# A bias table built with copies on GpSimd instead of matmuls on TensorE

## The chip, the cores and the metric

One core of a Trainium2 chip runs the whole program. The metric is device time in microseconds (us); the time before is the median of three runs. Engines are named as in the profile: PE is TensorE (PEld its weight loads), DVE VectorE, ACT ScalarE, POOL GpSimd, and SP the sync engine, whose queue issues nearly all of this kernel's DMAs.

## The reference

A bidirectional encoder of two layers works on 256 tokens of width 1024. Each layer has a token mixer and a gated MLP. The mixer projects the normed tokens to pooling channels, queries, keys, values and gates. Attention has three groups of four heads with strides 1, 4 and 16; each group adds a bias by relative position, in T5 buckets, the same in both layers. Cut to what the change touches:

```python
def _t5_buckets(rel):                       # 32 buckets
    n = -rel
    half = N_BUCKETS // 2
    ret = (n < 0).astype(np.int32) * half
    n = np.abs(n)
    max_exact = half // 2
    large = max_exact + (np.log(np.maximum(n, 1) / max_exact)
                         / np.log(MAX_DISTANCE / max_exact) * (half - max_exact)).astype(np.int32)
    large = np.minimum(large, half - 1)
    return (ret + np.where(n < max_exact, n, large)).astype(np.int32)
...
    for gi, (window, dilation) in enumerate(ATTN_GROUPS):
        hs = slice(gi * HEADS_PER_GROUP, (gi + 1) * HEADS_PER_GROUP)
        half = window // (2 * dilation)
        buckets = _t5_buckets(dilation * np.arange(-half, half + 1))
        bias = rel_bias[buckets][:, hs].T
        o_g, lse_g = _dilated_group(q[:, :, hs], k[:, :, hs], v[:, :, hs], bias, window, dilation)
```

In `_dilated_group` the bias is added to the logits, and positions outside the window or the sequence are set to -1e30.

## The kernel before

Tokens are held as two sets of 128, even and odd ones. All big products run on PE with each weight split into a high part (cast by ACT, line 177 or 185) and a rest (subtracted by DVE, line 178 or 186), in pieces. Class `Weights` keeps the order of the pieces. A DMA of 1 MB (line 117, tile `raw`, three buffers) loads two pieces; `W.get` splits up to three pieces ahead, with five buffers of split pieces; a raw buffer comes free when its second piece is split, and then the next load can go.

The program text of layer 0 has this order: the values of x (lines 654 and 741, first piece groups scaled by the norm's gain on the way), the parameters (`load_params`, lines 341 to 350), the bias table (`load_bias`, then the generator `build_bias`), the gain of norm2 (line 290), eight pooling projections (line 484) with their window sums on DVE (lines 814 to 836), the query and key projections, with the pooling output `pool_ps` among them, and the attention steps. The text's order is a priority only: a scheduler orders each engine's instructions and each queue's DMAs by its own reckoning of when their data is ready. `tc.issue_after(ins)` adds, to each instruction traced in the block on the engine of `ins`, an edge behind it; `W.behind[1]` is a DVE instruction, the last scaled subtraction of the first stage.

POOL does little: in each norm it adds up the sums of squares and takes the power that gives `rstd` (lines 423 to 428, in the first norm 628 to 631). Line 719 spreads that `rstd` over partitions with PE (`r_ps`).

**The bias table.** Head h and distance kind n (five kinds: even to even, two odd ones, stride 4, stride 16) need, for each of 255 distances, the bias of its bucket or a large negative number. `_bias_table` holds 33 rows of 5 x 256: row b has a 1 where bucket b applies, row 32 the mask. Before, these 33 rows come in by a DMA (`onehot_sb`), ACT casts them (`ohr`), the 32 x 12 biases come in as `rb` with a 33rd row of ones, DVE splits them into `rh` and `rl`, and PE multiplies: two matmuls of 4 x 256 for each kind into `f_ps` (line 374), copied by DVE to `fsb` (line 378). A `yield` follows each kind, and each pooling projection of layer 0 calls `next(bias)` first, so that one kind stands before each of the first five projections and the rest before the sixth:

```python
        fd = dram.tile([1, n], F32, name="fd")
        nc.sync.dma_start(out=fd[0].rearrange("(h e) -> h e", h=HPG), in_=fsb)
        sk = dram.tile([P, n + 1], F32, name="sk")
        nc.sync.dma_start(out=sk[:, 0:n], in_=fd[0].partition_broadcast(P))
```

This is the way through DRAM (lines 383 and 385): the 20 KB go to `fd`, then 128 times to `sk` (2.5 MB), and five DMAs (line 390) read them back with a row pitch that shifts each partition by one, into `bt`, which the scores read (line 885, first at 112.5 us).

Three tags of the pool `big` matter: `m2` holds pieces of the first values, then `ohr`, then `po2` and `m2`; `ybig` and `q1` held `onehot_sb` and `fsb` between other tiles.

Of the kernel before, what the change touches and what calls it, by code (L numbers as in the profile page):

```python
# [10 lines left out]
F32 = mybir.dt.float32  # L11
F32R = mybir.dt.float32r
# [4 lines left out]
P = 128  # L17
# [5 lines left out]
HPG = 4  # L23
NG = 3
NH = HPG * NG
# [8 lines left out]
NT = 5  # L34
# [10 lines left out]
def _buckets(rel):  # L45
    n = -rel
    ret = (n < 0).astype(np.int32) * 16
    n = np.abs(n)
    large = 8 + (np.log(np.maximum(n, 1) / 8) / np.log(1024 / 8) * 8).astype(np.int32)
    large = np.minimum(large, 15)  # L50
    return (ret + np.where(n < 8, n, large)).astype(np.int32)


def _bias_table():

    t = np.zeros((33, NT, 256), np.float32)
    delta = np.arange(255) - 127
    for n, (e, dil) in enumerate(
        ((2 * delta, 1), (2 * delta + 1, 1), (2 * delta - 1, 1), (2 * delta, 4), (2 * delta, 16))
    ):  # L60
        valid = (e % dil == 0) & (np.abs(e) <= 64 * dil)
        b = _buckets(e)
        j = np.nonzero(valid)[0]
        t[b[j], n, j] = 1.0
        t[32, n, np.nonzero(~valid)[0]] = NEG
        t[32, n, 255] = NEG
    return t.reshape(33, NT * 256)


def _edge_table():  # L70
# [134 lines left out]
def encoder(ctx, tc, x, w_in, w_pool, pool_scale, w_a, w_b, w_o, norm1, norm2, w_up, conv_w,  # L205
            conv_b, w_down, rel_bias, norm_f, onehot, edges, out):
    nc = tc.nc
    const = ctx.enter_context(tc.tile_pool(name="const", bufs=1))
    wpool = ctx.enter_context(tc.tile_pool(name="weights", bufs=1))
    big = ctx.enter_context(tc.tile_pool(name="big", bufs=1))  # L210
    sm = ctx.enter_context(tc.tile_pool(name="small", bufs=2))
    acc = ctx.enter_context(tc.tile_pool(name="acc", bufs=4, space=bass.MemoryType.PSUM))
# [6 lines left out]
    def cols(w, c0):  # L219

        src = w[:, c0 : c0 + 256].rearrange("(k p) c -> p k c", p=P)
        return W.add(
            src, (8, 256), [((lambda t, j=j: t[:, :, j * P : (j + 1) * P]), (8, P)) for j in (0, 1)]
        )
# [10 lines left out]
    for l in range(DEPTH):  # L235
        for g in range(NG):
            c0 = C_V + g * 512
            slots = (("m2", 0, 2), ("m2", 1, 2), ("ybig",), ("at2",)) if g == 0 else ()
            for j in range(2):
                tag = "k1" if l == 0 and g == 1 and j == 0 else None  # L240
# [34 lines left out]
        for f in range(0, NF, 2):  # L275
            a = cols(w_up[l], f * P) if f >= ENTRY else []
            g = cols(w_up[l], DFF + f * P)
# [7 lines left out]
    h = const.tile([P, 2, D], F32, name="h")  # L285
    xv = x[0].rearrange("(m t) d -> m t d", t=2)

    def gain(src):
        g = sm.tile([P, D], F32, tag="gain", bufs=1, name="gain")
        nc.sync.dma_start(out=g, in_=src.partition_broadcast(P))  # L290
        return g
# [47 lines left out]
    def load_params():  # L339

        nc.sync.dma_start(out=edge.rearrange("p a b -> p (a b)"), in_=edges[0].partition_broadcast(P))
        for l in range(DEPTH):
            rowst = sm.tile([96, P], F32, tag="s", name="prow")
            nc.sync.dma_start(out=rowst[0:66, :], in_=conv_w[l].rearrange("w (f p) -> (w f) p", p=P))
            nc.sync.dma_start(out=rowst[66:88, :], in_=conv_b[l].rearrange("(f p) -> f p", p=P))
            nc.sync.dma_start(out=rowst[88:96, :], in_=pool_scale[l].rearrange("(f p) -> f p", p=P))
            pt = mmp.tile([P, 512], F32, tag="mm", name="prm_ps")
            nc.tensor.transpose(pt[:, :96], rowst, ident[:96, :96])
            nc.vector.tensor_copy(prm[:, l, :], pt[:, :96])
            nc.vector.tensor_scalar_mul(hps[:, l, :], prm[:, l, 88:96], 0.5)  # L350

    bt = const.tile([P, HPG, NT * P], F32, name="bt")

    def load_bias():
        oh = big.tile([33, NT * 256], F32, tag="ybig", name="onehot_sb")
        nc.sync.dma_start(out=oh, in_=onehot)
        rb = sm.tile([33, NH], F32, tag="rb", bufs=1, name="rb")
        nc.vector.memset(rb, 1.0)
        nc.sync.dma_start(out=rb[0:32, :], in_=rel_bias)
        rh = sm.tile([33, NH], F32R, tag="ms", name="rh")  # L360
        rl = sm.tile([33, NH], F32R, tag="ms", name="rl")
        nc.vector.tensor_copy(rh, rb)
        nc.vector.tensor_sub(out=rl, in0=rb, in1=rh.bitcast(F32))
        ohr = big.tile([33, NT * 256], F32R, tag="m2", name="onehot_r")
        nc.scalar.copy(out=ohr, in_=oh)
        return rh, rl, ohr

    def build_bias(rh, rl, ohr):

        fsb = big.tile([HPG, NT * 256], F32, tag="q1", name="fsb")  # L370
        for n, g in enumerate((0, 0, 0, 1, 2)):
            ps = acc.tile([P, 512], F32, tag="acc", name="f_ps")
            for j, r in enumerate((rh, rl)):
                nc.tensor.matmul(
                    ps[:HPG, :256], r[:, g * HPG : (g + 1) * HPG], ohr[:, n * 256 : (n + 1) * 256],
                    start=(j == 0), stop=(j == 1),
                )
            nc.vector.tensor_copy(fsb[:, n * 256 : (n + 1) * 256], ps[:HPG, :256])
            yield

        n = HPG * NT * 256
# [4 lines that stand above are left out]
        for blk, kind in enumerate((2, 0, 1, 3, 4)):  # L386
            src = bass.AP(
                sk.tensor, sk.offset + kind * 256 + 127, [[n, P], [NT * 256, HPG], [1, P]]
            )
            nc.sync.dma_start(out=bt[:, :, blk * P : (blk + 1) * P], in_=src)  # L390
        yield
# [179 lines left out]
    def v_tile():  # L571
        return acc.tile([P, 512], F32, tag="acc", name="v_ps")
# [176 lines left out]
    for l in range(DEPTH):  # L749
# [25 lines left out]
        else:  # L775
            for g in range(NG):
                held = begun[0] if g == 0 else [W.get() for _ in range(4)]
                for t in range(2):
                    if g + t == 0:
                        ps = begun[1]  # L780
                    else:
                        ps = v_tile()
# [6 lines left out]
        if l == 0:  # L789
            load_params()  # L790
            with tc.issue_after(W.behind[1].ins):
                bias = build_bias(*load_bias())
        g2 = gain(norm2[l])


# [4 lines left out]
        for gi in range(3, -1, -1):  # L800
# [8 lines left out]
            cur, n = u, S + 2 * PAD  # L809
            sh = 1  # L810
            while sh < w:
# [3 lines left out]
                    out=nxt[:, :, 0:n], in0=cur[:, :, 0:n], in1=cur[:, :, sh : sh + n]  # L815
# [7 lines left out]
            if hw > 1:  # L823
                e = edge[:, gi, hw : w - 1].unsqueeze(1).to_broadcast([P, 2, hw - 1])
                r = slice(o + S - hw + 1, o + S)
# [3 lines left out]
                out=pd, in0=cur[:, :, o : o + S], scalar=1.0 / w, in1=u[:, :, PAD : PAD + S],  # L829
# [108 lines left out]
        for pair in ((0, 1), (2, 3)):  # L938
            a, b = pair
# [8 lines left out]
        for m, c in enumerate(PAIRS):  # L948
# [7 lines left out]
            for n in range(4):  # L956
# [5 lines left out]
                if hd < HPG:  # L962
# [3 lines left out]
                        out=lo[:, hd], in0=src, scalar=scale, in1=hi[:, hd].bitcast(F32),  # L966
# [3 lines left out]
                        out=lo[:, hd], in0=rest, scalar=scale, in1=lo[:, hd].bitcast(F32),  # L970
                        op0=ALU.mult, op1=ALU.add,
                    )
                else:
# [3 lines left out]
                        out=o, in0=src, scalar=scale, in1=o, op0=ALU.mult, op1=ALU.add  # L977
# [20 lines left out]
        for c in range(KD):  # L998
            th = gate(c)
            nc.vector.scalar_tensor_tensor(  # L1000
                out=pa[:, c, :], in0=th, scalar=1.0, in1=pa[:, c, :], op0=ALU.add, op1=ALU.mult
            )
        m2 = big.tile([P, 2, KD, 2, P], F32R, tag="m2", name="m2")
        mh, ml = m2[:, 0], m2[:, 1]
        for c4 in range(2):
            ths = [gate(4 * c4 + j) for j in range(4)]
            for j2 in range(2):
                i, (wh, wl) = W.get()
                for j in range(2):
                    c = 4 * c4 + 2 * j2 + j  # L1010
                    ps = mmp.tile([P, 2, S], F32, tag="mm", name="b_ps")
# [5 lines left out]
                        out=m, in0=ths[2 * j2 + j], scalar=1.0, in1=m, op0=ALU.add, op1=ALU.mult  # L1017
# [49 lines left out]
        held, ps = entry  # L1067
        first = keep_entry(ps)
        ps = v_tile()
# [106 lines left out]
```

## Time and profile before

| | before |
|---|---|
| median of three runs | 880.66 us (880.24 to 880.85) |
| the profiled execution | 880.48 us, of which span 878.7 us |
| granted TensorE clock | 0.998 |
| PE busy | 870.6 us, 4817 matmuls |
| DVE busy | 684.3 us, 1167 instructions |
| ACT busy | 524.1 us, 929 instructions |
| POOL busy | 14.1 us, 40 instructions |
| f_ps (line 374) | 10 matmuls, 43.5 to 55.2 us |
| fd, sk, first bt issued | 56.98, 60.89, 74.55 us |

The span runs from the first to the last instruction; the run's time has 1.78 us more around it. In the views, a line gives the start or the busy time in us, the engine, the line of the kernel, the operation, out<-in and a count; a bracket is idle time before it and what ended that. PEld is the weight load of a matmul and overlaps PE. A time of a DMA issue on SP (SPq) is that of the issuing, not of the transfer.

### The profile page before, as it was taken

The numbers are of one execution on the slowest core, as the hardware profiler recorded it, in microseconds if no ns is written. First come the engines' busy times: TensorE is split into PE (matmuls) and PEld (weight loads), VectorE is DVE, ScalarE is ACT, GpSimd is POOL, SyncE is SP. The second block draws the span as 40 slices with busy tenths as digits, with TensorE's granted clock in tenths as the row PEclk, the third lists the DMA queues.
The fourth block names the chain that finished last, engine by engine and source line by source line (L and its number), as shares of the span: only waits on it lengthen the run. The fifth ranks groups of instructions, "written<-read, shape, count | busy, mean of one in ns | idle before, by whom it ended". The sixth has DMA issues, their size and how long they took to land.

```text
span 878.7 us, 12698 instructions
## 1 busy us (share of the span) xinstructions
PE 870.6 (99%) x4817; PEld 756.5 (86%) x4817; DVE 684.3 (78%) x1167; ACT 524.1 (60%) x929; POOL 14.1 (2%) x40
## 2 busy tenths in 40 slices
PE   9999999999999999999999999999999999999996
PEld 7888889988888888888888888899888888888885
DVE  7987886766869987787755987776678698877874
ACT  7745654556647766666545565554666486656662
POOL 2000000000000000000000000000000000000000
PEclk9999999999999999999999999999999999999999
DMA  9669744454565465465636465443556447456441
GB/s 336 229 204 290 261 145 149 140 186 158 187 211 194 143 239 193 145 232 198 240 120 223 161 197 187 149 162 125 188 191 213 152 151 252 168 192 212 171 144 49
DMA packets 125790, 164.47 MB, mean 187 GB/s; under 512 B 2995, under 2 KB 106107, under 8 KB 125600
## 3 DMA queue, kind: packets, MB, share of 16 engines
q1 hardware_dynamic: 125712, 163.65, 55.5%
q8 instruction: 38, 0.62, 0.3%
q14 instruction: 24, 0.20, 0.1%
q10 hardware_dynamic: 16, 0.00, 0.0%
HBM read 162.57 MB, written 3.69 MB: 189 GB/s over the span
## 4 chain that ended last, share of the span: by engine, by line
PE 99%; ACT 0%; issue 0%; POOL 0%; DVE 0%; POOLq 0%; ACTq 0%
PE proj_ps L484 61%; PE v_ps L579 6%; PE res_ps L510 6%; PE res_ps L511 6%; PE res_ps L509 6%; PE b_ps L484 3%; PE v_ps L741 2%; PE v_ps L654 1%; PE pool_ps L484 1%; PE s_ps L879 1%; PE o_ps L929 1%; PE pt_ps L908 1%; PE s_ps L874 1%; PE o_ps L925 1%; PE xt_ps L450 1%; PE gain_ps L333 0%
## 5 line engine op out<-in xcount | busy, mean ns | idle before, releaser
L178 DVE TENSOR_TENSOR wl<-raw,wh 128x1024 fp32r<-128x1024 f32 x274 | 334.0, 1223 | 87.1 <-ACT wh L177 85.0
L484 PE MATMUL proj_ps<-x,wh 128*128 128x512 f32 x1408 | 360.0, 393 | 0.0
L177 ACT CAST wh<-raw 128x1024 fp32r<-128x1024 f32 x274 | 286.4, 1050 | 80.4 <-PE res_ps L511 39.1
L484 PEld LDWEIGHTS proj_ps<-x,wh 128*128 128x128 f32 x1408 | 257.5, 188 | 47.3 <-issue 0.7
L484 PEld LDWEIGHTS proj_ps<-x,wl 128*128 128x128 f32 x1408 | 192.6, 190 | 10.6
L484 PE MATMUL proj_ps<-x,wl 128*128 128x256 f32 x1408 | 196.7, 283 | 0.0
L509 PE MATMUL res_ps<-wh,actq 128*128 128x512 f32 (+1 forms) x184 | 70.0, 380 | 0.0
L510 PE MATMUL res_ps<-wl,actq 128*128 128x512 f32 (+1 forms) x184 | 69.9, 380 | 0.0
L511 PE MATMUL res_ps<-wh,actk 128*128 128x512 f32 (+1 forms) x184 | 69.9, 380 | 0.0
L1089 ACT ACTIVATE y<-a,prm 128x256 f32<-128x256 f32 x36 | 21.6, 601 | 40.3 <-DVE a L505 40.3
L509 PEld LDWEIGHTS res_ps<-wh,actq 128*128 128x128 f32 x184 | 34.6, 188 | 6.6
L510 PEld LDWEIGHTS res_ps<-wl,actq 128*128 128x128 f32 x184 | 34.6, 188 | 6.6
L511 PEld LDWEIGHTS res_ps<-wh,actk 128*128 128x128 f32 x184 | 34.6, 188 | 6.5
L484 PE MATMUL proj_ps<-po,wh 128*128 128x512 f32 x128 | 34.0, 400 | 0.0
L1090 DVE SCALAR_TENSOR_TENSOR y<-a,prm,y 128x255 f32<-128x255 f32 x36 | 17.4, 483 | 14.2 <-ACT y L1089 14.2
L484 PEld LDWEIGHTS proj_ps<-po,wh 128*128 128x128 f32 x128 | 23.1, 189 | 3.9
L509 PE MATMUL res_ps<-wh,m 128*128 128x512 f32 (+1 forms) x72 | 26.5, 368 | 0.0
L511 PE MATMUL res_ps<-wh,m 128*128 128x512 f32 (+1 forms) x72 | 26.3, 365 | 0.0
L510 PE MATMUL res_ps<-wl,m 128*128 128x512 f32 (+1 forms) x72 | 26.3, 365 | 0.0
L579 PE MATMUL v_ps<-wh,x 128*128 128x512 f32 x80 | 25.7, 392 | 0.0
L416 ACT ACTIVATE junk<-h 128x512 f32<-128x512 f32 (+1 forms) x20 | 10.9, 546 | 24.7 <-DVE h L414 24.7
L995 ACT ACTIVATE gates<-gates 128x256 f32<-128x256 f32 x32 | 13.1, 415 | 18.9 <-DVE gates L505 18.9
(208 smaller groups left out, 1111.0 us busy)
## 6 DMA issues: line engine op xcount, KB each, us to landing
raw<-in_w_in_dram SPq DMA_DIRECT2D x58, 1024.0 KB, 5.6
raw<-in_w_up_dram SPq DMA_DIRECT2D x44, 1024.0 KB, 5.1
raw<-in_w_down_dram SPq DMA_DIRECT2D x22, 1024.0 KB, 5.0
raw<-in_w_a_dram SPq DMA_DIRECT2D x8, 1024.0 KB, 5.1
raw<-in_w_o_dram SPq DMA_DIRECT2D x8, 1024.0 KB, 5.0
raw<-in_w_b_dram SPq DMA_DIRECT2D x4, 1024.0 KB
sk<-fd SPq DMA_DIRECT2D x1, 2560.0 KB
raw<-in_w_pool_dram SPq DMA_DIRECT2D x2, 1024.0 KB
```

Source lines behind the costliest of these rows:

```text
L177: lambda: nc.scalar.copy(out=h, in_=src),
L178: lambda: nc.vector.tensor_sub(out=l, in0=src, in1=h.bitcast(F32)),
L416: nc.scalar.activation(junk[:, 0 : cc.stop - cc.start], h[:, t, cc], AF.Square, scale=D**-0.5, accum_out=ss[:, n : n + 1],)
L484: nc.tensor.matmul(out, w(k), x, start=(n == 0), stop=(n == 2 * nk - 1))
L509: nc.tensor.matmul(ps, ah, wh, start=first, stop=False)
L510: nc.tensor.matmul(ps, ah, wl, start=False, stop=False)
L511: nc.tensor.matmul(ps, al, wh, start=False, stop=last)
L579: nc.tensor.matmul(ps, x2[:, 2 * n + j, part, t, :], w[:, j, :], start=(n + m == 0), stop=(n == 3 and m == 5),)
L741: nc.tensor.matmul(ps[t], a[:, k, t, :], w[:, j, :], start=(k + m == 0), stop=(k == KD - 1 and m == 2),)
L995: nc.scalar.activation(th, th, AF.Tanh, scale=0.5)
L1089: nc.scalar.activation(y, a, AF.Identity, bias=b, scale=w1)
L1090: nc.vector.scalar_tensor_tensor(out=y[:, 1:], in0=a[:, : S - 1], scalar=w0, in1=y[:, 1:], op0=ALU.mult, op1=ALU.add)
```

## The change

The matmuls that build the table, their inputs and their copies go. Instead the biases are loaded turned, four heads on four partitions (`rbt`, three small DMAs), and row 32, the mask, is loaded onto the four partitions of `fsb`. POOL then copies, for each run of places that share a bucket, that bucket's bias over the run: 15, 16, 15 and 11 runs in the kinds 0, 1, 3 and 4, of 1 to 22 elements; kind 2 is one copy of kind 1, moved by a place. `fsb` lies in `m2` instead of `q1`. The generator now yields six times, the first of them taken at once, so that the way through DRAM stands before the sixth pooling projection in the text as it did before.

```diff
+def _runs(n):
+
+    t = _bias_table()[:32].reshape(32, NT, 256)[:, n]
+    runs = []
+    for b in range(32):
+        places = np.nonzero(t[b])[0]
+        if len(places):
+            step = int(places[1] - places[0]) if len(places) > 1 else 1
+            assert (np.diff(places) == step).all()
+            runs.append((b, int(places[0]), len(places), step))
+    return runs
...
-    def load_bias():
-        oh = big.tile([33, NT * 256], F32, tag="ybig", name="onehot_sb")
-        nc.sync.dma_start(out=oh, in_=onehot)
-        rb = sm.tile([33, NH], F32, tag="rb", bufs=1, name="rb")
-        nc.vector.memset(rb, 1.0)
-        nc.sync.dma_start(out=rb[0:32, :], in_=rel_bias)
-        rh = sm.tile([33, NH], F32R, tag="ms", name="rh")
-        rl = sm.tile([33, NH], F32R, tag="ms", name="rl")
-        nc.vector.tensor_copy(rh, rb)
-        nc.vector.tensor_sub(out=rl, in0=rb, in1=rh.bitcast(F32))
-        ohr = big.tile([33, NT * 256], F32R, tag="m2", name="onehot_r")
-        nc.scalar.copy(out=ohr, in_=oh)
-        return rh, rl, ohr
-
-    def build_bias(rh, rl, ohr):
-
-        fsb = big.tile([HPG, NT * 256], F32, tag="q1", name="fsb")
-        for n, g in enumerate((0, 0, 0, 1, 2)):
-            ps = acc.tile([P, 512], F32, tag="acc", name="f_ps")
-            for j, r in enumerate((rh, rl)):
-                nc.tensor.matmul(
-                    ps[:HPG, :256], r[:, g * HPG : (g + 1) * HPG], ohr[:, n * 256 : (n + 1) * 256],
-                    start=(j == 0), stop=(j == 1),
+    def build_bias():
+        rbt = sm.tile([HPG, NG, 32], F32, tag="rb", bufs=1, name="rbt")
+        fsb = big.tile([HPG, NT, 256], F32, tag="m2", name="fsb")
+        for g in range(NG):
+            with nc.allow_non_contiguous_dma("a small table, turned"):
+                nc.sync.dma_start(
+                    out=rbt[:, g], in_=rel_bias[:, g * HPG : (g + 1) * HPG].rearrange("b h -> h b")
                 )
-            nc.vector.tensor_copy(fsb[:, n * 256 : (n + 1) * 256], ps[:HPG, :256])
+        nc.sync.dma_start(
+            out=fsb.rearrange("p a b -> p (a b)"), in_=onehot[32].partition_broadcast(HPG)
+        )
+        for n, g in ((0, 0), (1, 0), (3, 1), (4, 2)):
+            for b, j, count, step in _runs(n):
+                nc.gpsimd.tensor_copy(
+                    fsb[:, n, j : j + (count - 1) * step + 1 : step],
+                    rbt[:, g, b : b + 1].to_broadcast([HPG, count]),
+                )
+
+        nc.gpsimd.tensor_copy(fsb[:, 2, 64:192], fsb[:, 1, 63:191])
+        fsb = fsb.rearrange("p a b -> p (a b)")
+        for _ in range(6):
             yield
...
             load_params()
             with tc.issue_after(W.behind[1].ins):
-                bias = build_bias(*load_bias())
+                bias = build_bias()
+                next(bias)
```

## The prediction

> **What bounds the kernel now.** I read the page first: engine shares and the chain that ended last.
>
> ```profile
> span 878.7 us, 12698 instructions
> PE 870.6 (99%) x4817; PEld 756.5 (86%) x4817; DVE 684.3 (78%) x1167; ACT 524.1 (60%) x929; POOL 14.1 (2%) x40
> PE 99%; ACT 0%; issue 0%; POOL 0%; DVE 0%; POOLq 0%; ACTq 0%
> ```
>
> PE is never without work once it has started, so an edit gains by what it takes out of PE's order and loses by any hole it tears there. POOL is almost unused. Next I read the chain in order of time around the bias build (start, length, what).
>
> ```profile
> 41.91 1.62 PE proj_ps L484 x7
> 43.54 0.32 PE f_ps L374 x2
> ...
> 45.56 2.99 PE proj_ps L484 x16
> 48.54 0.33 PE f_ps L374 x2
> ...
> 55.16 0.32 PE f_ps L374 x2
> 55.48 22.50 PE proj_ps L484 x128
> ...
> 79.38 2.79 PE proj_ps L484 x16
> ```
>
> The five f_ps pairs are on the path, and a projection beside one takes 2.97 to 2.99 us where an undisturbed one takes 2.79. Third, the DMA queue of SP, in order of time (start, length, issue).
>
> ```profile
> 20.79 0.36 SPq L290 DMA_DIRECT2D gain<-in_norm_dram  x1
> ...
> 55.48 0.37 SPq L117 DMA_DIRECT2D raw<-in_w_pool_dram  x1
> 56.98 0.28 SPq L383 DMA_DIRECT2D fd<-fsb  x1
> 60.89 0.59 SPq L385 DMA_DIRECT2D sk<-fd  x1
> 63.94 0.39 SPq L117 DMA_DIRECT2D raw<-in_w_in_dram  x1
> 74.55 3.28 SPq L390 DMA_DIRECT2D bt<-sk  x5
> 77.94 32.74 SPq L117 DMA_DIRECT2D raw<-in_w_in_dram  x9
> ```
>
> Two things are to be seen. The way through DRAM (fd, sk, bt) holds SP from 57 to 78 us with one weight load let through. And SP's order is not the order of the program text: the gain of norm2 stands behind the whole value stage in the text (PE ends that at 41.7) and goes out at 20.79. The scheduler puts a transfer where it reckons its data ready.
>
> Last, what POOL does beside DVE (all engines, around 435 us).
>
> ```profile
> 434.44 1.23 DVE L178 TENSOR_TENSOR wl<-raw,wh 128x1024 fp32r<-128x1024 f32 x1 [0.69 <-ACT wh L177]
> 435.11 0.63 POOL L423 TENSOR_SCALAR ss<-ss 128x1 f32<-128x1 f32 x1 [176.18 <-ACT junk L416]
> 437.26 0.19 POOL L425 TENSOR_TENSOR ss<-ss 128x1 f32<-128x1 f32 x1 [1.52 <-ACT junk L416]
> 437.53 0.57 POOL L428 TENSOR_TENSOR rstd<-ss,mhalf 128x1 f32<-128x1 f32 x1
> ```
>
> The L423 instruction takes 0.22 us when DVE is idle (250.04, 440.94). Here it took 0.63 and ended at 435.74, 0.07 after DVE's subtraction of two SBUF operands (435.67). At 10.31 two of them took 2.01 us beside such DVE work. So a POOL instruction waits out a DVE instruction that reads two SBUF operands; DVE's own 1.23 is its usual length.
>
> **What is removed.** Ten matmuls in five places. From the first projection (41.91) to 55.48 are 13.57 us with 64 projection matmuls; at 2.79 for 16 these cost 11.16. The five pairs therefore cost 2.41 us, 1.61 as f_ps and 0.80 in the changeovers; with the slower pace of the next stretch (22.50 for 128) it is 2.32. I take 2.4. Also gone are DVE's five copies (0.41 each), its memset, cast and subtraction (0.4), and ACT's cast of 1.26: all beside PE, counted at nothing, since the weights they could hasten are split 8 us ahead there (the piece split until 55.41 is used by the projection of about 63.9). The onehot and rb loads go too.
>
> **What is added on SP.** Three small turned loads and the mask row, for two loads removed: two issues more, at 0.28 to 0.42 us each, 0.7 us. They fall before 23.92, ahead of which SP waits 2.8 us for a free raw buffer (gain's issue ends at 21.15): nothing, and 0.7 if that cover were gone. Their transfers are small; what the element-wise reads cost is between 0 and some microseconds of a few DMA engines, against first use of raw loads of that time at 32.5. I take nothing.
>
> **What is added on POOL.** 15, 16, 15 and 11 runs of a bucket and one copy: 58 instructions. No copy is in this trace. Bounds for one: 0.03 us apart (the constant memsets at the start) and 0.97 (the mean of L628); the nearest rows are L425, 0.20 long, and L425 to L428, 0.28 from start to start. I take 0.20, and 0.10 (the memsets' length) and 0.28 as ends. They start at about 25.5: the mask issued at about 21.5 and 3.6 to 3.9 to land, as fd and the gain show. From 25.5 to 56.6 DVE spends 21.4 us in two-operand SBUF instructions (L186 5.5, L178 9.8, L729 2.6, L814 2.8, L828 0.7), 25 of them, which leaves 9.6 us. Letting POOL take one copy behind each such instruction and the beat in the free stretches, the 58 are done at 40 (0.10), 49 (0.20) or 56 us (0.28). I take 49. At 0.97 it would be 82. If each copy held DVE up for the 0.07 seen above, that would be 58 x 0.07 = 4 us of DVE, of which PE would feel what its lead doesn't cover, 0 to 4; the DVE rows beside POOL show no lengthening, so I take 0.
>
> The Trainium skill, GPSIMD Engine Reference, Specifications, says that POOL's SBUF interfaces are shared with VectorE, with contention against DVE instructions that have two SBUF inputs or run in a 2-port mode. The trace agrees with it by the 0.63 against 0.22 above; the rule alone gives no length, and it speaks against this change by making the copies last longer.
>
> **What is moved.** fsb moves into m2, free since PE's last use of it, over at about 14 us, and next written at 82.4: no wait. q1 loses fsb: no one waited. The text place of fd, sk and bt stays the sixth projection. fd now waits for POOL, and behind fd in SP's queue stand sk, bt and every later weight load; behind those ACT's casts, then PE. The cover that matters: the load issued at 63.94 landed at 77.05 behind sk, its cast ended at 78.10 and PE took it at 78.98, a lead of 0.9 us. If fd keeps its place behind the load of 55.48 and that load moves with PE, lead and gain stay. If that load does not move, fd goes at 55.9 instead of 57.0, sk 1.1 earlier, PE 2.4 earlier: a hole of 0.4. If fd goes earlier and finds POOL done, sk is out of the way sooner. Sum: 2.0 to 2.4 us less, I take 2.4: the profiled execution would go from 880.48 (span 878.7 and 1.78 around it) to 878.1, the median from 880.66 to 878.3. About 0.2%, 1.8 us, is what a measurement can tell from no change, so this is just outside.
>
> **Rival 1, slower: SP stands at fd before POOL is done.** The scheduler pulls fd forward to where it reckons the copies done without DVE's interference: 25.5 + 58 x 0.2 = 37. POOL really ends at 49. fd goes then, sk 3.9 later (as from 56.98 to 60.89) at 53, and a load behind sk at 53.3 lands 13.1 later (63.94 to 77.05) and is cast at 67.5. If it is the load that went at 38.69 before, the seventh projection wants it at 61.1 - 2.4 = 58.7: a hole of 8.8. If that one slips in between and the next (42.7 before) is behind, the ninth wants it at 64.3: a hole of 3.2. Net 0.8 to 6.4 us slower; I put it at 884.3. A hole opens once POOL ends after 40.2 in the first order or 45.8 in the second, and 2.4 us later the gain is used up. For it: the 20.79 row and the contention rows. Against: a beat of 0.10, or a scheduler that reckons copies as slow as they are.
>
> **Rival 2, about the same: the copies get ahead of rstd.** POOL's rstd of 16.92 to 17.86 feeds r_ps, which PE reaches at 19.59. If copies are put ahead of it while the mask, issued at 14.8, lands only at 18.5 to 22.1 (3.7, or the 7.3 of the weight loads then), rstd (0.64 + 0.94 = 1.6) ends at 20.1 to 23.7: a hole of 0.5 to 4.1, net 1.9 faster to 1.7 slower; 880.3. For it: POOL is idle from 13.25 to 16.20. Against: the DMA engines are full then, so the mask is hardly reckoned there that early.
>
> **Rival 3, nothing gained:** the weights set PE's pace and a hole opens where f_ps was; 880.7. Against it the 8 us lead above.
>
> **Chances.** Forecast 0.47. Rival 1 0.32, of which 0.05 within 0.2%. Rival 2 0.11: 0.06 same, 0.05 slower. Rival 3 0.03, same. POOL slower still (beyond 56 us, up to the 82), so that fd is late even at its old place, each microsecond behind 55.5 costing one: 0.07 slower. Together faster 0.47, same 0.14, slower 0.39. Range: from 877.6 (changeovers dearer than reckoned, a gain of 3.1) to 887.0 (the upper end of rival 1); the forecast's own is 877.8 to 878.8.
>
> **What would show it.** Right: no f_ps on the chain, eight pooling projections without gaps at 2.79 to 2.81, POOL's last copy near 49, fd right behind it, no PE wait until 100 us. Rival 1: a long wait of SP at fd for POOL, then ACT's casts waiting for raw and a PE gap between 56 and 80. Rival 2: POOL waiting for a DMA ahead of rstd and PE waiting at r_ps. Copies of over 0.3 us, or DVE subtractions longer than 1.22, would make the sum wrong.

## The result and the profile after

The changed kernel takes 892.05 us (median of four runs, 891.57 to 892.76) against 880.75 for the kernel before: 11.3 us slower, ratio 1.0129 (95% interval 1.0117 to 1.0141). The forecast was 878.3. The busy times on the page of the changed kernel (span 890.4 us), and the shares of the chain that ended last:

```profile
PE 871.0 (98%) x4807; PEld 758.2 (85%) x4807; DVE 682.2 (77%) x1159; ACT 523.5 (59%) x928; POOL 29.3 (3%) x98
PE 93%; DMA 3%; POOL 2%; ACT 0%; DVE 0%; SPq 0%; issue 0%; POOLq 0%; ACTq 0%; DVEq 0%
```

PE lost its ten matmuls, and DMA and POOL are now on the chain. The chain in order of time shows where (start, length, what):

```profile
41.28 0.23 POOL fsb L388
...
41.53 1.87 DMA fd<-fsb
...
44.10 14.73 DMA raw<-in_w_in_dram
...
58.93 1.05 ACT wh L190
...
60.03 30.21 PE proj_ps L496 x160
90.25 1.40 PE pool_ps L496 x8
```

Read from the bottom: PE resumes at 60.03 because ACT's cast ended then; the cast had waited for a weight load, issued at 44.10 and on its way for 14.73 us, since it stood behind `sk`; `sk` waited for `fd`, and `fd` for POOL's last copy at 41.5. The queue of SP shows why the load was so late (start, length, issue). First the same load in the kernel before, then the changed kernel:

```profile
33.76 0.37 SPq L117 DMA_DIRECT2D raw<-in_w_in_dram  x1
```

```profile
24.39 0.39 SPq L130 DMA_DIRECT2D raw<-in_w_in_dram  x1
24.83 0.57 SPq L303 DMA_DIRECT2D gain<-in_norm_dram  x1
41.53 0.28 SPq L395 DMA_DIRECT2D fd<-fsb  x1
43.41 0.59 SPq L397 DMA_DIRECT2D sk<-fd  x1
44.10 22.67 SPq L130 DMA_DIRECT2D raw<-in_w_in_dram  x5
```

`fd` stands right behind the gain's load. From 25.4 to 41.5 SP issues nothing, and the weight load that went at 33.76 in the kernel before goes at 44.10, 10.3 us later. That is about half of the delay. ACT cast these weights at 39.06 in the kernel before, so their way took 5.3 us at most (39.06 - 33.76); here it took 14.73, with the 2.5 MB of `sk` ahead of it. The cast starts at 58.93, 19.9 us later than before. The waits (who, for whom, total us, times, longest):

```profile
SPq L395 <- POOL fsb L388: 16.0, 1, 16.0
PE proj_ps L496 <- ACT wh L190: 11.9, 1, 11.9
```

The stretches by granted clock (stretch, its length, then PE, PEld, DVE, ACT and POOL busy, PEclk, DMA share, GB/s) show a second loss:

```profile
48.00:50.00 2.00, 0.09 (x1) 0.00 (x0) 0.00 (x0) 0.00 (x0) 0.00 (x0) 1.00 1.07 326
50.00:60.00 10.00, 0.00 (x0) 0.00 (x0) 0.00 (x0) 1.07 (x2) 0.00 (x0) 0.55 0.97 292
...
61.00:62.00 1.00, 1.00 (x4) 0.75 (x3) 1.00 (x2) 0.28 (x2) 0.00 (x0) 0.50 1.09 387
...
64.00:65.00 1.00, 1.00 (x9) 1.00 (x8) 1.00 (x2) 0.00 (x0) 0.00 (x0) 0.71 0.99 316
65.00:66.00 1.00, 1.00 (x10) 0.95 (x9) 1.00 (x2) 0.81 (x2) 0.00 (x0) 1.00 1.07 381
```

PE comes out of the hole at a granted clock of 0.50 and has 1.00 again only from 65. Until the first `pool_ps` the terms add up: a hole of 11.95; the ten projections behind it at 30.21 instead of 27.90 (160 matmuls at the 33.48 for 192 of an undisturbed run, below), 2.3; the two projections ahead of the hole at 5.84 (42.24 to 48.08) instead of 5.58, 0.26; a first projection that starts 0.33 later (42.24 for 41.91); less 2.6 for the matmuls: 12.25. Measured there: 90.25 - 77.98 = 12.27. At the end it is 890.4 - 878.7 = 11.7; where the rest of the span gives back the 0.6 was not followed up.

### The profile page after: what moved, and what is told of

Read it like the earlier page. It is cut to its first block, busy times and chain, and to the rows that moved or that the text cites. A ratio compares the mean times of both kernels' runs of the same rounds, so it can differ in the third digit from the quotient of the medians.

```text
span 890.4 us, 12733 instructions
## 1 busy us (share of the span) xinstructions
PE 871.0 (98%) x4807; PEld 758.2 (85%) x4807; DVE 682.2 (77%) x1159; ACT 523.5 (59%) x928; POOL 29.3 (3%) x98
## 4 chain that ended last, share of the span: by engine, by line
PE 93%; DMA 3%; POOL 2%; ACT 0%; DVE 0%; SPq 0%; issue 0%; POOLq 0%; ACTq 0%; DVEq 0%
PE proj_ps L496 60%; PE v_ps L591 6%; PE res_ps L522 6%; PE res_ps L523 6%; PE res_ps L521 6%; DMA raw<-in_w_in_dram 3%; PE b_ps L496 3%; POOL fsb L383 2%; PE pool_ps L496 1%; PE o_ps L942 1%; PE s_ps L892 1%; PE pt_ps L921 1%; PE s_ps L887 1%; PE o_ps L938 1%; PE xt_ps L462 1%; DMA fsb<-in_onehot_dram 0%
## 5 line engine op out<-in xcount | busy, mean ns | idle before, releaser
L496 PE MATMUL proj_ps<-x,wh 128*128 128x512 f32 x1408 | 360.9, 394 | 11.9 <-ACT wh L190 11.9
L435 POOL TENSOR_SCALAR ss<-ss 128x1 f32<-128x1 f32 x8 | 2.0, 255 | 819.4 <-ACT junk L428 819.4
```

Source lines behind the costliest of these rows:

```text
L496: nc.tensor.matmul(out, w(k), x, start=(n == 0), stop=(n == 2 * nk - 1))
```

## The experiments

Each kernel is compared with the kernel before on the same chip (880.63 to 880.84 us). Two theories were set against each other. **Queue**: SP stands at `fd` until POOL is done, and the weight loads behind it come late. **Contention**: it isn't the wait, but POOL beside DVE, the small turned loads, or `sk`'s traffic at that time, that makes the weights late.

**The change with `fd` held back.** `W.load` keeps the DMA it issued last as `self.last`, and `fd` gets an edge behind it:

```diff
-        nc.sync.dma_start(out=fd[0].rearrange("(h e) -> h e", h=HPG), in_=fsb)
+        with tc.issue_after(W.last.ins):
+            nc.sync.dma_start(out=fd[0].rearrange("(h e) -> h e", h=HPG), in_=fsb)
```

> The change, with one edge added: fd may go out on SP only behind the weight load that was traced last before it (the one that went at 47 us in the kernel before). Queue theory (SP stood at fd for POOL and held the weights back): POOL is done at 41.5, fd finds it done, no hole at the third projection, and the 2.4 us of the bias matmuls show: 878.3, between 877.8 and 879.0. Contention theory (POOL beside DVE, or the turned loads, delay the weights whatever SP does): the hole stays at least in part, over 881. If the matmuls' removal is worth nothing: 880.7.

878.14 us, ratio 0.9972 (0.9964 to 0.9980). `fd` goes without a wait for POOL, which ended at 43.0:

```profile
46.57 0.43 SPq L396 DMA_DIRECT2D fd<-fsb  x1
```

One edge on one DMA takes back 13.9 us; POOL's copies and the turned loads are all still there. So contention from these falls, and the gain is near the forecast's (2.7 us for 2.4) once SP doesn't wait at `fd`. The profiled execution, one of the twelve runs and at 881.72 the longest, had a wait of PE at the pooling output:

```profile
PE proj_ps L497 <- DVE po L867: 2.6, 1, 2.6
```

It is the same kind of wait, only smaller: SP stood 7.6 us at the first `bt` for `sk`, and the weight load behind `bt` went at 72.21 and was cast at 80.45; DVE's rest of that piece stood ahead of the pooling output. It isn't the load right behind `sk`, for which the forecast had reckoned its lead of 0.9 us. The short hole also cost more than itself: PE resumed at a granted clock of 0.50, and the projection there took 4.41 us instead of 2.79.

**No copies.** The 58 copies are left out, so the table holds the mask alone; `fd` keeps its early place.

```diff
-        for n, g in ((0, 0), (1, 0), (3, 1), (4, 2)):
-            for b, j, count, step in _runs(n):
-                nc.gpsimd.tensor_copy(
...
-        nc.gpsimd.tensor_copy(fsb[:, 2, 64:192], fsb[:, 1, 63:191])
```

> The change without POOL's 58 copies, so that the table holds the mask alone; fd keeps its early place on SP, ahead of the second weight load. Queue theory: fd waits only for the mask (landed at 25.4), sk goes at about 27.5, the load behind it at 28 lands some 14.7 later at 43, ahead of the 47 at which the third projection wants its cast weights: no hole, 878.3 (up to 880 if the early sk makes a small one). Rival (the early 2.5 MB of sk are what delays the weights, not the wait): the hole stays, 886 or more.

877.56 us, ratio 0.9966 (0.9953 to 0.9979). SP's queue behind the gain's load, which goes at 24.34:

```profile
25.01 0.28 SPq L387 DMA_DIRECT2D fd<-fsb  x1
30.14 0.58 SPq L389 DMA_DIRECT2D sk<-fd  x1
34.08 19.28 SPq L130 DMA_DIRECT2D raw<-in_w_in_dram  x5
```

The order is that of the changed kernel, but `fd` goes at once, and the load behind it goes at 34.08, as early as its buffer allows. An early `sk` of 2.5 MB opens no hole by itself; the wait in front of it did. But it uses up the lead: the load behind it landed at 45.53, and the cast of its first piece ended at about 46.6 for a projection that starts at 47.6. No run has the wait without `sk` ahead of the load, so the half of the delay that is `sk`'s way is read from the traces, not tested apart.

**Copies twice.**

```diff
-            for b, j, count, step in _runs(n):
+            for b, j, count, step in _runs(n) * 2:
```

> The change with each of the 57 bucket copies done twice, the result unchanged; fd keeps its early place. Queue theory: each microsecond that POOL takes longer is a microsecond of PE hole. The second set finds DVE idle for want of weights and runs at 0.13 us each, 7.4 us: POOL done at about 49, total about 899.5. Rival (POOL's length doesn't matter): 892.

899.81 us, ratio 1.0217 (1.0204 to 1.0230), against the 899.5 reckoned. `fd` goes at 48.26 instead of 41.53, 6.7 us later; the total is 7.8 us longer, PE's hole 19.5 instead of 11.9. The ten projections behind the hole take 30.92 instead of 30.21. The place of `fd` in the queue is the same with no copies, 58 and 115.

**The way through DRAM on POOL's queue.** `fd`, `sk` and `bt` are issued by `nc.gpsimd` instead of `nc.sync`.

> The change with fd, sk and bt issued from POOL's own queue, so that POOL waits for itself and SP carries weights only. Queue theory: no hole from waiting; sk shares the DMA engines with the weight loads between 42 and 60, which may cost 0 to 2: 878.3 to 880.3. Rival (sk's traffic delays the weights by itself): a hole of 4 or more, 883 and up.

878.74 us (877.79 to 882.83), ratio 0.998 (0.9969 to 0.9991). No hole where it was; PE waits 0.4 us once after its start, at the pooling output. SP then carries weights only, and POOL waits for itself. The runs spread more than those with the edge.

**Where `fd` goes.** Three versions of the kernel with the edge, each with another number of yields (one of the three new lines), so that `fd` stands behind another load:

```diff
-        for _ in range(6):
+        for _ in range(7):   # fd behind the pooling weights' load
+        for _ in range(4):   # one load earlier than with 6
+        for _ in range(2):   # two loads earlier than with 6
```

> The version with the edge, with fd put one load later: behind the load of the pooling weights, the order of SP's queue as in the kernel before. POOL is long done. My prediction's own cover is at test: if that load moves along with the earlier PE, no hole and 878.0; if the lead of 0.9 us behind sk is used up, a hole of 0.4 to 1.5 and 878.5 to 879.7. Contention or matmuls worth nothing: 880.7.

878.15 us, ratio 0.9968 (0.9956 to 0.9980). In the profiled execution PE waits 0.5 us at the pooling output, again for the load behind `bt`: SP stood 10.2 us at `bt` for `sk`, and that load went at 74.85.

> The version with the edge, with fd one load earlier than in the first such run: behind the load of about 42.7. POOL done by then or within 0.3 us; sk goes between 45 and 50. Queue theory: 877.6 to 878.2, within 0.3 us of the run with fd two loads earlier.

877.90 us, ratio 0.9968 (0.9955 to 0.9980).

> The version with the edge, with fd put two loads earlier: behind the load that went at about 38.7, ahead of the next two. POOL ends near 42.5, the next load's buffer is free at about the same time, so fd holds SP 0 to 3 us; sk goes at 45 and is through by 59, long before the weights of the pooling output. Queue theory: as in the run without copies, 877.6 (877.4 to 878.2). If 3 us at fd open a hole: 879 or more.

877.79 us (877.62 to 878.01), ratio 0.9967 (0.9954 to 0.9979). SP waits 3.7 us for POOL at `fd` and loses nothing by it, since the buffer of the load behind it came free only shortly before. The chain in order of time:

```profile
41.94 33.48 PE proj_ps L497 x192
```

Twelve projections run from 41.94 without anything between, at 2.79 each, and `pool_ps` starts at 75.41 against 77.98 before. This is the best full version of the set, 3.0 us ahead of the kernel before and 14.3 ahead of the changed one; the three places of `fd` with the full table lie within 0.4 us of each other.

**Memsets for copies.** POOL's 58 copies are replaced by memsets over the same places, which read nothing; the biases are left out of the table.

```diff
-                nc.gpsimd.tensor_copy(
-                    fsb[:, n, j : j + (count - 1) * step + 1 : step],
-                    rbt[:, g, b : b + 1].to_broadcast([HPG, count]),
-                )
+                nc.gpsimd.memset(fsb[:, n, j : j + (count - 1) * step + 1 : step], 0.5)
```

> The change with POOL's 58 copies replaced by 58 memsets over the same places, which read nothing (the biases are left out of the table); fd keeps its early place. If it is POOL's reading that waits for DVE, the memsets run at 0.03 to 0.13 each, POOL is done at 27 to 32 and the hole is 0 to 2: 877.6 to 880. If POOL's writes are held by DVE too, POOL still ends near 41 and the total stays at 892.

878.46 us (877.59 to 878.82), ratio 0.9973 (0.9962 to 0.9984). The instructions of `fsb`, first in the changed kernel, then with memsets (count, then shortest, median and longest in ns, first and last start):

```profile
L383 POOL COPY fsb<-rbt x57: 175/182/2988, 25.5 to 41.1; 4x1 f32<-4x1 f32 x21, 4x6 f32<-4x6 f32 x6, 4x2 f32<-4x2 f32 x6, 4x3 f32<-4x3 f32 x4
```

```profile
L383 POOL MEMSET fsb<- x57: 88/91/111, 25.0 to 27.0; 4x1 f32 x21, 4x6 f32 x6, 4x2 f32 x6, 4x3 f32 x4
```

The same writes take 2.1 us instead of 15.8, and none is longer than 0.11. They are done before most of the DVE work that the copies met, so only the start can be compared: while DVE computes `xu` and `x` in both kernels (lines 735 and 741 of the changed one, the second with two inputs in SBUF), 57 memsets go in 2.1 us and 13 copies in 2.6. So POOL's reading waits for DVE there, and its writing doesn't.

**The text's place.** The changed kernel without the edge, with eight yields instead of six.

> The change with the way through DRAM written two projections later in the text (eight yields instead of six) and no edge. If the text's place decides where fd goes on SP, fd comes after 50 us, finds POOL done, and the total is 878. If fd goes out as soon as its producers stand in POOL's order, wherever the text has it, fd stays right behind the gain's load at 24.8, and the total stays at 892 (891 to 893).

891.36 us, ratio 1.0124 (1.0107 to 1.0141). `fd` stands right behind the gain's load again and goes at 41.30. Two projections later in the text did not move it.

## Why the prediction was wrong

**The step that failed is the place of `fd` in SP's queue, and with it the wait of SP at `fd`, which the forecast's sum put at nothing.** The forecast had `fd` behind the load of 55.48, or earlier with POOL done. It stood behind the gain's load of 24.83 instead; SP waited 16.0 us there for POOL, and PE's hole was 11.95. From the gain's load at 20.79 I had read that the scheduler puts a transfer where it reckons its data ready, and in rival 1 I reckoned that for `fd` as 37 us, from the copies' length. The runs show that the length doesn't enter: with 0, 58 and 115 copies, with memsets, and with the text's place two projections later, `fd` stood at the same point, behind the gain's load. By which rule the scheduler puts it there stays open; a place as soon as the producers stand in their engine's order would fit all five, and wasn't tested apart from them. In the kernel before, `fd`'s producers were DVE copies behind matmuls that stood between PE's projections, and `fd` came when the fifth was done.

**Rival 1 named the mechanism and missed its size.** It had 884.3, up to 887, for a hole of 3.2 to 8.8 at the seventh or ninth projection. The hole was 11.95 at the third: the load that stood behind `fd` and `sk` was the one of 33.76, not that of 38.69, and feeds the third projection, which PE reaches at 48. Its way behind `sk` was 14.73 instead of 13.1. And no term of mine held what a hole costs afterwards, here 2.3 us at a granted clock of 0.50. That the forecast's 878.3 comes near the versions in which SP doesn't wait bears out its term for the matmuls, not its reading of the queue.

**What was removed**: reckoned at 2.4, measured at 2.6 between the first projection and `pool_ps` (36.07 before, 33.47 in the best version), 2.9 over the whole span. That is more than the 1.61 of the matmuls alone, so the changeovers count, as the forecast had them.

**POOL's length**: 49 was forecast for its end, with 40 to 56 as ends; it came at 41.5. The beat is 0.13 us when DVE is idle (the last 11 bucket copies took 1.42), near the lower end of 0.10 and not the 0.20 that I took from its nearest row. The holding by DVE is real, and in one place harder than one copy behind each DVE instruction: the first of these three copies took 2.99 us, from 36.51 to 39.50, and spans two subtractions of DVE, which end at 39.45:

```profile
36.51 3.26 POOL L383 COPY fsb<-rbt 4x6 f32<-4x6 f32 x3
37.10 2.35 DVE L191 TENSOR_TENSOR wl<-raw,wh 128x1024 fp32r<-128x1024 f32 x2
```

DVE itself took 2.35 for the two, as in the kernel before (2.36): it isn't slowed, which was the 0 I had taken. One of the rows from which the prediction took that POOL waits for DVE was misread: at 440.94 in the kernel before DVE was not idle, but ran line 544 (`h<-res_ps,h`, one input in PSUM) until 441.07, and POOL's 0.22 was not lengthened by it. The Trainium skill, SBUF — State Buffer, Who interferes with whom, says that a DVE instruction with two SBUF inputs contends with a GpSimd instruction that reads SBUF, not with one that only writes it. The memsets agree with that: 0.091 against 0.182 us in the median and 0.111 against 2.988 at the longest.

**Right as reckoned**: the additions on SP (the three turned loads end at 22.0, the weight load behind them goes at 24.39, and with `fd` out of the way they cost nothing that shows) and the place of `fsb` in `m2`. The hole of 0.4 that the forecast allowed for at the pooling output came out as 0.5 with `fd` at its old place, but for another load, so that this nearness is luck. Rival 2 did not occur: POOL's copies begin at 25.47, behind both `rstd`. Rival 3 is refuted by the 2.6.

## What to carry to other kernels

Before moving work to an idle engine, look at what waits for it and in which queue: here 16 us on an idle engine were free, and the one small DMA that waited for them held every weight load behind it, and the large `sk` that depended on it then went ahead of those loads. A transfer that depends on a slow producer needs a queue of its own, or an edge that keeps it behind the loads that are due first; where its text stands is no such edge. When an engine looks as if it ran free beside DVE, ask what it reads: writes went at 0.09 us each, reads were held up to 3 us.

## What the runs showed of the hardware

A hole cost PE more than its length, and the addition did not grow in step with the hole. It follows how long PE, back at work, still had a granted clock of 0.50 (the moments are worked out from its mean in stretches of 1 or 2 us):

| run | hole, us | back at work until the clock rose, us | projections behind it, us | loss, us |
|---|---|---|---|---|
| the changed kernel | 11.95 | 4.5 | 30.21 instead of 27.90 | 2.3 |
| text's place | 12.1 | 3.0 | 29.54 instead of 27.90 | 1.6 |
| copies twice | 19.5 | 6.1 | 30.92 instead of 27.90 | 3.0 |
| `fd` held back, the longest run | 2.6 | 3.0 | 4.41 instead of 2.79 | 1.6 |

The loss is about half of that time in all four. The wait of 0.5 us in the run with `fd` behind the pooling weights' load left the clock at 1.00. In the changed kernel PE stopped at 48.08 and the clock fell at about 50.9; in the run with the hole of 2.6 us it stopped at 80.96 and the clock fell at about 83.1, 2.2 us later; in the run with the text's place it stopped at 47.59 and the clock fell at about 52.5, 4.9 us later. The Trainium skill, TensorE: Matmul & The Clock Gate, What's actually happening, gives half the clock after an idle window of about 3.4 us, and the full one after about as long a busy stretch. The runs agree with it only roughly: the clock fell after 2.2 to 4.9 us, and the way back took 3.0 to 6.1. The price of a hole is to be reckoned with that addition; here a hole of 2.6 us already paid it.
